# The second pass of the sample's attention scores as two 64-row matmuls side by side in the array

## The chip, the cores and the metric

The kernel runs on one core of one Trainium2 chip. The metric is the device time of one execution in microseconds (us); the median of three runs before the change is 1824.78 us (1824.75 to 1825.05). The engines are named as the profile names them: PE is TensorE (PEld its weight loads), DVE VectorE, ACT ScalarE, POOL GpSimd, SP the engine that issues the transfers.

## The reference, cut to what matters

One layer of a bidirectional encoder is applied to two sequences with the same weights, a prompt of 512 tokens and a sample of 1024. Width 1024, 8 query heads and 2 key/value heads of 64, MLP width 4096, all in float32.

```python
q = _axial_rope(_rmsnorm(q, q_g), ang_row, ang_col)
k = _axial_rope(_rmsnorm(k, k_g), ang_row, ang_col)
...
s = jnp.einsum('bqkgd,bskd->bkgqs', qi, k).astype(jnp.float32) * scale
p = jax.nn.softmax(s, axis=-1).astype(v.dtype)
return jnp.einsum('bkgqs,bskd->bqkgd', p, v)
...
h = h + jnp.concatenate([o_attn, o_pool], axis=-1) @ w_out
h = h + jnp.square(jax.nn.relu(m @ w_up)) @ w_down
```

The score of a query and a key is a product over the 64 numbers of a head. All sequences are attended to in full, without a mask.

## The kernel before, in words

Tokens are cut into 12 tiles of 128 (tiles 0 to 3 are the prompt, 4 to 11 the sample) and into three chunks of 512 (chunk 0 the prompt, 1 and 2 the sample). PE multiplies in the type float32r, which keeps fewer bits than float32. So every operand is stored as a high part (the rounded value) and a low part (the rest), and a product is made of several float32r products added up in PSUM.

For the scores the two parts are packed differently. A head has 64 numbers, the array 128 rows. `turn_qk` (line 327) writes the tile `qs` so that the high part of a head's q stands on 64 partitions and its low part on the other 64; heads with an even number have the high part on partitions 0 to 63, odd ones on 64 to 127. The tile goes to memory (`qs_d`), and `load_q` (line 402) brings it back as `qb`, one tile of tokens ahead of its use. The keys are stored as `ks[c][0]` (high part) and `ks[c][1]` (low part) of chunk c, and both repeat the head's 64 numbers on both halves of the partitions. One matmul over 128 rows of `qb` against `ks[c][0]` thus gives (q high + q low) times k high, a second one against `ks[c][1]` gives (q high + q low) times k low.

`Unit.score` (line 433) issues these for one head of one tile: for a prompt tile one chunk, two matmuls of 512 columns; for a sample tile two chunks, four matmuls, into one PSUM tile `S` of two banks. DVE then takes the row maximum (`nm`, line 441), ACT the exponentials (`soften`, 449), DVE the reciprocal of their sum, POOL the scaling (`norm`, 461), PE turns the weights (`turn`, tile `tp`), ACT and DVE split them (`split`, 472 and 473), PE multiplies them with v (`weigh`, tile `o`).

The order of all this is written out by hand in one loop (line 992), and PE, ACT, DVE and POOL execute it in that order. A unit is one tile and one key/value head, and each of its four steps handles one query head: in each step of the sample PE gets four score matmuls (`S`), four matmuls of `weigh` for work of earlier steps (`o`), eight transposes (`tp`) and, while there is such work, a piece of filling: six matmuls of the pooling heads' output projection (`pp`) or twelve of 256 columns of the attention heads' (`po`, lines 738 to 753). I call a step with a piece `po` filled and one without any unfilled. The sample has 8 tiles, 2 units each, 4 steps each: 64 steps.

Most tiles in the on-chip memory come from one pool of 49 equal slots (`slot`, line 74). All transfers are issued by SP, in order; `load` (line 55) also keeps a load behind the PE instruction before it in program order. Every matmul issued goes through `pe.matmul` (line 49), so the profile gives all of them that line and tells them apart by tile.

Of the kernel before, what the change touches and what calls it, by code (L numbers as in the profile page):

```python
# [10 lines left out]
F32R = mybir.dt.float32r  # L11
# [7 lines left out]
P = 128  # L19
# [3 lines left out]
NQ, NKV, HD = 8, 2, 64  # L23
# [3 lines left out]
SEQS = ((0, 4), (4, 8))  # L27
NT = 12
NF = 32
CH = 512  # L30
# [5 lines left out]
def encoder_layer(ctx, tc, xT, xn, xr, pT, w1, w2, w_pool, w_out, w_up, w_down, w_gate, w_proj,  # L36
# [18 lines left out]
    def load(dst, src):  # L55
        ins = sy.dma_start(dst, src).ins
        if last_pe[0] is not None:
            tc.add_manual_dep(ins, last_pe[0].name, NOSYNC, reason="not before its turn")

    def as32(ap):  # L60
        return ap.bitcast(F32)
# [12 lines left out]
    def slot(shape, dt, name):  # L74
        n = math.prod(shape[1:])
        full = slots.tile([P, SLOT], dt, tag="s", name=name)
        v = full[:, 0:n]
        if len(shape) == 3:
            v = v.rearrange("p (a b) -> p a b", a=shape[1])
        elif len(shape) == 4:  # L80
            v = v.rearrange("p (a b c) -> p a b c", a=shape[1], b=shape[2])
        return v

    def tp_ps(name):
        return pst.tile([P, CH], F32, tag="tp", name=name)
# [21 lines left out]
    qs_d = [dram.tile([P, NQ * P], F32, name=f"qs_d{t}") for t in range(NT)]  # L107
# [135 lines left out]
    ks, vs, uT = {}, {}, {}  # L243
# [153 lines left out]
        ve.scalar_tensor_tensor(y[:, 1], py, psc_sb[:, g:g + 1], as32(y[:, 0]), op0=ALU.mult, op1=ALU.subtract)  # L397
        sy.dma_start(yT_d[c][g], flat(y))

    qsb = {}  # L400

    def load_q(t):
        qsb[t] = slot([P, NQ, P], F32R, f"qb{t}")
        load(as32(qsb[t]).rearrange("p h t -> p (h t)"), qs_d[t])


    fill = deque()
# [12 lines left out]
    class Unit:  # L420
# [12 lines left out]
        def score(self, j, tag="s"):  # L433
            hq, nch = self.g * 4 + j, self.nc
            S = ps(tag, f"S{self.id}{j}") if tag == "s" else tp_ps(f"S{self.id}{j}")
            for c in range(nch):
                for i in range(2):
                    pe.matmul(S[:, c * CH:(c + 1) * CH], qsb[self.t][:, hq % 2 * 4 + hq // 2, :], ks[self.t0 // 4 + c][i][:, self.g, :],
                              start=i == 0, stop=i == 1)
            nm = small.tile([P, 1], F32, tag="nm", name=f"nm{self.id}{j}")  # L440
            ve.tensor_reduce(nm, S[:, :nch * CH], axis=AX.X, op=ALU.max, negate=True)
            self.S[j] = S, nm
# [448 lines left out]
    def stream():  # L891

        for n, pr in enumerate(pairs):
            for i, _ in enumerate(pr.feed()):
# [5 lines left out]

    unit = Unit(0, 0, 0)
    first = {(10, 6): [lambda: load_q(0)],
             (10, 7): [lambda: load_wo(4), lambda: load_wo(5)],
             (11, 0): [lambda: load_wo(6), lambda: load_wo(7)],
# [3 lines left out]
             (11, 4): [lambda: load_pool(0), lambda: load_h(0, 0), lambda: unit.norm(0), lambda: split_wo(6, ve)],  # L908
             (11, 5): [lambda: unit.score(1, "tp"), lambda: split_wo(7, ve)],
             (11, 6): [lambda: load_q(1)]}  # L910
    start_chunk(0)
    for k in range(KD - 2):
# [79 lines left out]
    for at in range(2, 4 * len(units) + 6):  # L992
        idx, j = divmod(at, 4)
        if j == 0:
            cur = Unit(*units[idx]) if idx < len(units) else None
            if cur and cur.g == 0 and cur.t + 1 < NT:
                load_q(cur.t + 1)
# [179 lines left out]
    for n, pair in enumerate(pairs):  # L1177
        c, g = pair.c, pair.g
# [215 lines left out]
```

## Time and profile before

| what | value |
|---|---|
| median of the runs | 1824.78 us |
| time of the profiled execution | 1827.95 us |
| its span, first to last instruction | 1826.2 us |
| PE busy | 1769.2 us, 97% |
| DVE busy | 1247.3 us, 68% |
| POOL busy | 1047.5 us, 57% |
| ACT busy | 939.5 us, 51% |
| granted TensorE clock, mean | 0.991 |
| score matmuls (`S`) | 320, from 181.9 to 542.8 us |

The profiled execution is one more run of the same program, 3.2 us above the median of the timed runs. Outside its span lie 1.75 us. A matmul's end is modelled in the profile, so durations of consecutive matmuls overlap; the pace of PE is read from the distance of starts. In a timeline the first number is the start and the second the length of a row of equal instructions, and the brackets say how long the engine had been idle and what it waited for.

### The profile page before, as it was taken

The page shows a single profiled execution, that of the slowest core. Times are in us where ns is not written, and L with a number is a line of the kernel's source. Part 1 is how long each engine was busy: PE and PEld are TensorE (multiplying, and loading weights), DVE is VectorE, ACT ScalarE, POOL GpSimd, SP SyncE. Part 2 cuts the span into 40 slices and gives each one's busy share as a digit, 9 for nine tenths or more (in the row PEclk, how much of TensorE's full clock was granted, in tenths as well). Part 3 has the DMA queues.
Part 4 walks back from the last instruction along what each step waited for, and adds up shares of the span by engine and source line. Part 5 has one row for each costly group of instructions (what it writes and reads, how often), then busy time and mean ns, then how long its engine had stood idle before and what let it go on. Part 6 is the DMA issues. An engine that isn't in the chain of part 4 may idle for free. (4 is left out here: it accounts for less than half of the span.)

```text
span 1826.2 us, 28559 instructions
## 1 busy us (share of the span) xinstructions
PE 1769.2 (97%) x10540; PEld 1543.7 (85%) x10540; DVE 1247.3 (68%) x1823; ACT 939.5 (51%) x1854; POOL 1047.5 (57%) x917
## 2 busy tenths in 40 slices
PE   9999899999998999999998999999999999999997
PEld 7888677888868898898987988898888898988787
DVE  5677865888894777755668777765776555665655
ACT  6333455768793456544445465545444544443332
POOL 3474774536574567866555668855576666543121
PEclk9999999999999999999999999999999999999998
DMA  6333544120619435533555425536442322272102
GB/s 246 116 131 110 198 170 176 36 93 18 214 41 366 154 122 183 192 110 101 179 217 202 150 93 196 184 111 243 164 141 93 110 98 93 93 260 69 58 12 81
DMA packets 83883, 256.84 MB, mean 141 GB/s; under 512 B 9888, under 2 KB 16416, under 8 KB 83744
## 3 DMA queue, kind: packets, MB, share of 16 engines
q1 hardware_dynamic: 83744, 255.02, 39.6%
q8 instruction: 83, 1.36, 0.3%
q14 instruction: 56, 0.46, 0.1%
HBM read 195.74 MB, written 59.24 MB: 140 GB/s over the span
## 5 line engine op out<-in xcount | busy, mean ns | idle before, releaser
L49 PE MATMUL pd<-r,wd 128*128 128x512 f32 x2304 | 572.2, 396 | 13.1 <-DVE r L885 11.8
L49 PEld LDWEIGHTS pd<-r,wd 128*128 128x128 f32 x2304 | 420.9, 189 | 104.5 <-DVE r L885 17.5
L786 POOL TENSOR_TENSOR w<-ws,w 128x512 fp32r<-128x512 f32 x192 | 269.5, 1408 | 232.3 <-ACT w L785 226.0
L786 POOL TENSOR_TENSOR w<-wur,w 128x512 fp32r<-128x512 f32 x144 | 212.8, 1488 | 141.8 <-ACT w L785 140.6
L836 DVE TENSOR_TENSOR h<-pd,h 128x1024 f32<-128x1024 f32 x192 | 233.8, 1217 | 86.4 <-PE pd L49 86.2
L785 ACT CAST w<-ws 128x512 fp32r<-128x512 f32 x192 | 118.5, 617 | 269.6 <-DVE ws L794 248.4
L461 POOL TENSOR_SCALAR pr<-pr,rr 128x512 f32<-128x512 f32 x160 | 111.1, 705 | 136.1 <-DVE rr L456 64.2
L49 PE MATMUL z<-w,x 128*128 128x512 f32 (+1 forms) x864 | 175.2, 359 | 0.5 <-DVE w L160 0.3
L816 DVE TENSOR_TENSOR wd<-wdr,wd 128x512 fp32r<-128x512 f32 x96 | 106.2, 1106 | 92.8 <-ACT wd L815 81.6
L49 PEld LDWEIGHTS pz<-mo,w 128*128 128x128 f32 x1152 | 151.6, 191 | 20.5 <-issue 12.4
L49 PEld LDWEIGHTS z<-w,x 128*128 128x128 f32 x864 | 143.0, 189 | 27.0 <-ACT w L159 2.0
L49 PE MATMUL pz<-mo,w 128*128 128x256 f32 x1152 | 154.9, 285 | 11.0 <-issue 8.9
L49 PE MATMUL pq<-mo,w 128*128 128x256 f32 x1152 | 154.2, 284 | 2.8 <-issue 2.0
L49 PE MATMUL px<-mo,w 128*128 128x256 f32 x1152 | 152.8, 282 | 0.0
L49 PEld LDWEIGHTS px<-mo,w 128*128 128x128 f32 x1152 | 147.0, 190 | 4.1
L49 PEld LDWEIGHTS pq<-mo,w 128*128 128x128 f32 x1152 | 144.8, 191 | 3.6 <-issue 3.6
L49 PE MATMUL pg<-hg,wg 128*128 128x512 f32 (+1 forms) x768 | 141.5, 339 | 0.2
L49 PEld LDWEIGHTS pg<-hg,wg 128*128 128x128 f32 x768 | 119.0, 188 | 18.0 <-DVE hg L1128 1.0
L472 ACT CAST pt<-tp 128x512 fp32r<-128x512 f32 x160 | 87.9, 591 | 88.9 <-PE tp L53 87.2
L816 POOL TENSOR_TENSOR wd<-wdr,wd 128x512 fp32r<-128x512 f32 x96 | 129.8, 1352 | 0.0
L473 DVE TENSOR_TENSOR pt<-tp,pt 128x512 fp32r<-128x512 f32 x160 | 104.1, 684 | 31.3 <-ACT pt L472 31.0
L885 DVE TENSOR_TENSOR r<-c,r 128x512 fp32r<-128x512 f32 x96 | 75.2, 788 | 72.6 <-ACT c L882 45.0
(195 smaller groups left out, 3021.6 us busy)
## 6 DMA issues: line engine op xcount, KB each, us to landing
wur<-in_w_up_dram SPq DMA_DIRECT2D x96, 512.0 KB, 4.1
wdr<-in_w_down_dram SPq DMA_DIRECT2D x96, 512.0 KB, 4.4
mo_d<-mm SPq DMA_DIRECT2D x84, 256.0 KB, 2.4
mo<-mo_d SPq DMA_DIRECT2D x42, 512.0 KB, 7.8
h_d<-h SPq DMA_DIRECT2D x16, 512.0 KB, 2.9
h<-h_d SPq DMA_DIRECT2D x16, 512.0 KB, 10.0
xn<-in_xn_dram SPq DMA_DIRECT2D x12, 512.0 KB, 6.3
qs_d<-qs SPq DMA_DIRECT2D x12, 512.0 KB, 3.0
```

The lines of the kernel that those rows point to most:

```text
L49: last_pe[0] = nc.tensor.matmul(*a, **k).ins
L461: gp.tensor_scalar(p, p, rr, 1.0, op0=ALU.mult, op1=ALU.mult)
L472: sc.copy(self.pt[kt][:, 0], tp)
L473: ve.tensor_tensor(self.pt[kt][:, 1], tp, as32(self.pt[kt][:, 0]), op=ALU.subtract)
L785: sc.copy(t[:, 0], x)
L786: gp.tensor_tensor(t[:, 1], x, as32(t[:, 0]), op=ALU.subtract)
L816: (gp, ve)[i].tensor_tensor(lo, self.dr[i][:, h], as32(hi), op=ALU.subtract)
L836: ve.tensor_tensor(h, pd.rearrange("p (a b) -> p a b", a=2), h, op=ALU.add)
L885: ve.tensor_tensor(self.r[i][:, 1], x, as32(self.r[i][:, 0]), op=ALU.subtract)
```

## The change

For sample tiles the loop over the passes is now outside the loop over the chunks. The first pass is unchanged, two matmuls over 128 rows with `ks[1][0]` and `ks[2][0]`. In the second pass each matmul has 64 rows: chunk 1 uses partitions 0 to 63, chunk 2 partitions 64 to 127. Both use a new tile `qh`, which holds the high part of q in both halves; so the second pass gives q high times k low, and the product of the two low parts is left out for the sample. The two 64-row matmuls lie in different row halves of the array and write different banks of `S`. `load_q` fills `qh` with four more transfers from `qs_d` for each of the 8 sample tiles.

```diff
     def load_q(t):
         qsb[t] = slot([P, NQ, P], F32R, f"qb{t}")
         load(as32(qsb[t]).rearrange("p h t -> p (h t)"), qs_d[t])
+        if t >= SEQS[1][0]:
+            qhi[t] = slot([P, NQ, P], F32R, f"qh{t}")
+            dst = as32(qhi[t]).rearrange("p h t -> p (h t)")
+            for half in (slice(0, HD), slice(HD, P)):
+                for e, src in enumerate((slice(0, HD), slice(HD, P))):
+                    load(dst[half, e * CH:(e + 1) * CH], qs_d[t][src, e * CH:(e + 1) * CH])
...
-            for c in range(nch):
-                for i in range(2):
-                    pe.matmul(S[:, c * CH:(c + 1) * CH], qsb[self.t][:, hq % 2 * 4 + hq // 2, :], ks[self.t0 // 4 + c][i][:, self.g, :],
-                              start=i == 0, stop=i == 1)
+            at = hq % 2 * 4 + hq // 2
+            for i in range(2):
+                for c in range(nch):
+                    rows, q = slice(0, P), qsb
+                    if i and nch == 2:
+                        rows, q = slice(c * HD, (c + 1) * HD), qhi
+                    pe.matmul(S[:, c * CH:(c + 1) * CH], q[self.t][rows, at, :],
+                              ks[self.t0 // 4 + c][i][rows, self.g, :], start=i == 0, stop=i == 1)
```

PE, in a filled step of tile 5, before the change: the end of a piece `po`, the four score matmuls, two of `weigh` and a pair of transposes. In the names, `ks1_0` is the high part of chunk 1's keys, `ks1_1` the low part.

```order
L49 MATMUL po03_3519<-cat0_0_2333,wo3_1_3324 128x256
L49 MATMUL S5_01_3537<-ks1_0_807,qb5_3145 128x512
L49 MATMUL S5_01_3537<-ks1_1_808,qb5_3145 128x512
L49 MATMUL S5_01_3537<-ks2_0_1404,qb5_3145 128x512
L49 MATMUL S5_01_3537<-ks2_1_1405,qb5_3145 128x512
L49 MATMUL o4_0_3395<-pt4_06_3513,vs2_1406 128x512 x2
```

The same place after the change:

```order
L49 MATMUL po03_3534<-cat0_0_2333,wo3_1_3334 128x256
L49 MATMUL S5_01_3552<-ks1_0_807,qb5_3150 128x512
L49 MATMUL S5_01_3552<-ks2_0_1404,qb5_3150 128x512
L49 MATMUL S5_01_3552<-ks1_1_808,qh5_3152 128x512
L49 MATMUL S5_01_3552<-ks2_1_1405,qh5_3152 128x512
L49 MATMUL o4_0_3405<-pt4_06_3528,vs2_1406 128x512 x2
```

The count of matmuls is the same, the middle two have changed places, and the last two read `qh` (their output, which the row shows, is still 128 by 512).

SP, where the query tiles 5 and 6 are loaded, before:

```order
L56 DMA qb5_3145<-qs_d5_78 128x1024
L56 DMA wor2_3216<-in_w_out_dram 128x1024
L56 DMA wor3_3296<-in_w_out_dram 128x1024
L735 DMA h_d2_3_315<-h23_3058 128x1024
L56 DMA qb6_3483<-qs_d6_79 128x1024
L707 DMA h_d0_0_304<-h00_1952 128x1024
```

And after:

```order
L56 DMA qb5_3150<-qs_d5_78 128x1024
L56 DMA qh5_3152<-qs_d5_78 64x512 x4
L56 DMA wor2_3226<-in_w_out_dram 128x1024
L56 DMA wor3_3306<-in_w_out_dram 128x1024
L745 DMA h_d2_3_315<-h23_3063 128x1024
L56 DMA qb6_3493<-qs_d6_79 128x1024
L56 DMA qh6_3495<-qs_d6_79 64x512 x4
L717 DMA h_d0_0_304<-h00_1952 128x1024
```

Four transfers of 64 by 512 stand behind each load of a sample tile's `qb`; what stood behind it follows them, in the same order.

## Rows read from the trace of the kernel before

**Rows 1.** The page's first part: busy time of each engine over the span, its share and the count of instructions.

```profile
PE 1769.2 (97%) x10540; PEld 1543.7 (85%) x10540; DVE 1247.3 (68%) x1823; ACT 939.5 (51%) x1854; POOL 1047.5 (57%) x917
```

**Rows 2.** Busy time of the engines in six stretches: the first sixteen filled steps, two unfilled ones, eight unfilled ones, the unfilled end of the sample, and the 40 us behind it. The columns are the stretch, its length, then busy time and count of PE, PEld, DVE, ACT and POOL, the granted clock of PE, the busy share of the DMA engines and GB/s.

```profile
326.00:393.00 67.00, 65.95 (x445) 59.29 (x444) 54.40 (x106) 45.08 (x108) 29.50 (x41) 1.00 0.13 46
393.00:399.00 6.00, 6.00 (x37) 5.15 (x36) 5.42 (x11) 4.83 (x13) 1.52 (x3) 1.00 0.73 261
432.00:457.00 25.00, 23.88 (x130) 17.87 (x129) 23.09 (x42) 23.09 (x56) 18.98 (x23) 1.00 0.03 11
491.00:544.00 53.00, 50.29 (x266) 36.99 (x264) 49.76 (x91) 49.04 (x117) 37.15 (x47) 1.00 0.24 91
560.00:580.00 20.00, 20.00 (x165) 19.52 (x164) 9.20 (x20) 4.25 (x8) 5.47 (x5) 1.00 1.02 389
580.00:600.00 20.00, 12.19 (x85) 11.97 (x84) 9.99 (x15) 5.74 (x12) 8.72 (x8) 0.77 1.00 402
```

**Rows 3.** The timeline of PE over two filled steps (start, length, instructions).

```profile
343.26 1.10 PE L49 MATMUL S<-ks,qb 128*128 128x512 f32 x4
344.20 1.09 PE L49 MATMUL o<-pt,vs 128*128 128x512 f32 x4
345.13 1.03 PE L53 MATMUL tp<-id_sb,pr 128*128 128x128 f32 x8
345.92 1.65 PE L49 MATMUL po<-cat,wo 128*128 128x256 f32 x12
347.41 1.09 PE L49 MATMUL S<-ks,qb 128*128 128x512 f32 x4
348.33 1.09 PE L49 MATMUL o<-pt,vs 128*128 128x512 f32 x4
```

**Rows 4.** The matmuls `po` in the stretch from 326 to 497 us, from the table of groups: count, busy time, mean length in ns, idle time of PE just before them. Under it the timeline of PE over the first sample steps, before that stretch and up to its beginning.

```profile
L49 PE MATMUL po<-cat,wo 128*128 128x256 f32 x384 | 53.4, 288 | 0.0
...
310.71 1.19 PE L49 MATMUL S<-ks,qb 128*128 128x512 f32 x4 [0.78 <-DVE h L733]
...
322.43 1.64 PE L49 MATMUL pp<-yb,wo 128*128 128x512 f32 x6
...
328.17 0.50 PE L49 MATMUL o<-pt,vs 128*128 128x512 f32 x1 [1.05 <-DVE pt L473]
```

**Rows 5.** The timeline of DVE in the filled step that begins at 343.26 us.

```profile
344.40 1.23 DVE L441 TENSOR_REDUCE nm<-S 128x1 f32<-128x1024 f32 x1 [0.52 <-PE S L49]
345.54 0.15 DVE L455 TENSOR_TENSOR rr<-sums 128x1 f32<-128x1 f32 x1
345.72 0.16 DVE L456 RECIPROCAL rr<-rr 128x1 f32<-128x1 f32 x1
346.43 1.29 DVE L473 TENSOR_TENSOR pt<-tp,pt 128x512 fp32r<-128x512 f32 x2 [0.55 <-ACT pt L472]
347.64 0.42 DVE L754 TENSOR_TENSOR h<-po,h 128x256 f32<-128x256 f32 x1
347.97 0.83 DVE L498 TENSOR_TENSOR ob<-o,ob 64x256 f32<-64x256 f32 x2
```

**Rows 6.** The timeline of PE over unfilled steps, in the last of the three unfilled stretches.

```profile
496.62 1.09 PE L49 MATMUL S<-ks,qb 128*128 128x512 f32 x4
...
499.34 1.10 PE L49 MATMUL S<-ks,qb 128*128 128x512 f32 x4
...
502.08 1.08 PE L49 MATMUL S<-ks,qb 128*128 128x512 f32 x4
503.49 1.25 PE L53 MATMUL tp<-id_sb,pr 128*128 128x128 f32 x8 [0.33 <-DVE pt L473]
504.50 1.17 PE L49 MATMUL o<-pt,vs 128*128 128x512 f32 x4
505.51 1.10 PE L49 MATMUL S<-ks,qb 128*128 128x512 f32 x4
507.19 1.25 PE L53 MATMUL tp<-id_sb,pr 128*128 128x128 f32 x8 [0.58 <-DVE pt L473]
```

**Rows 7.** The instructions on the tile `S`: shortest, median and longest duration in ns, first and last start in us.

```profile
L49 PEld LDWEIGHTS S<-ks,qb x320: 186/188/338, 181.9 to 542.5; 128*128 128x128 f32 x160
L49 PE MATMUL S<-ks,qb x320: 386/393/714, 181.9 to 542.8; 128*128 128x512 f32 x160
```

**Rows 8.** The transfers into `qb`: the issue on SP in ns with first and last start, and the time to landing.

```profile
L56 SPq DMA_DIRECT2D qb<-qs_d x12: 320/378/644, 176.4 to 492.2; - x12
DMA to landing us min/median/max: 3.3/4.1/8.6
```

**Rows 9.** What stands on SP behind the last load of `qb`, and where PE next needs it: the timeline of SP, then of PE.

```profile
492.24 0.38 SPq L56 DMA_DIRECT2D qb<-qs_d  x1
492.73 2.31 SPq L56 DMA_DIRECT2D h<-h_d  x4
...
548.89 1.67 PE L49 MATMUL po<-cat,wo 128*128 128x256 f32 x12
```

**Rows 10.** The longest stall of PE behind the sample's attention: the timeline of PE, then that of DVE.

```profile
585.81 1.58 PE L49 MATMUL pq<-mo,w 128*128 128x256 f32 x12
595.21 2.90 PE L49 MATMUL pz<-mo,w 128*128 128x256 f32 x12 [7.82 <-issue]
...
591.48 1.23 DVE L661 TENSOR_TENSOR h<-h,w 128x1024 f32<-128x1024 f32 x1 [9.54 <-DMA h_d<-h]
```

More of the change, by code (lines that the diff above doesn't have):

```diff
@@ L398, in pool_product @@
         sy.dma_start(yT_d[c][g], flat(y))
-    qsb = {}
+    qsb, qhi = {}, {}
     def load_q(t):
```

## The prediction

> **What bounds the kernel now.** I read the page's first part, then the busy time by stretch, then the timelines of PE and DVE over single steps. The page says that PE is busy 97% of the span [rows 1], so PE's own pace is what a change can win or lose almost everywhere. For the sample's attention that has to be seen step by step. In the first sixteen filled steps PE is busy 65.95 of 67 us, DVE 54.40, ACT 45.08 [rows 2]: PE sets the pace. A filled step lasts from one group `S` to the next, 343.26 to 347.41, 4.15 us, and PE goes through its four groups without a bracket of idle time [rows 3]. Read from the starts: four `S` 0.94 us (0.92 in the next step), so 0.233 us each; eight transposes 0.79 us, 0.099 each; twelve `po` 1.49 us. DVE does 1.23 + 0.15 + 0.16 + 1.29 + 0.42 = 3.25 us in such a step, in one of four 0.83 more, and it is DVE that waits for PE's `S` (0.52 us) and for ACT (0.55 us) [rows 5]. So there is room of about 0.7 us before DVE would take over.
>
> In unfilled steps it is the other way. They begin at 2.72 and 2.74 us (496.62, 499.34, 502.08), which is PE's own sum, and then stretch to 3.43 us with PE waiting 0.33 and 0.58 us for DVE's `pt` [rows 6]. DVE's work in such a step is 1.23 + 0.15 + 0.16 + 1.29, plus a quarter of 0.83, 3.04 us. In the eight steps from 432 us and in the end of the sample DVE is busy 23.09 of 25 and 49.76 of 53 us [rows 2]. There, a faster PE waits more and gains nothing.
>
> The number of filled steps: 384 matmuls `po` between 326 and 497 us, twelve a piece, 32 pieces [rows 4]. Of the other 32 sample steps four, from 310.71 us on, hold the last pooling pieces (to 322.43), and 28 are unfilled.
>
> **The change part by part.** *The first pass* keeps its two matmuls, 2 x 0.233 = 0.466 us. That they now stand next to each other changes no pace: within and between the groups of rows 3 the distance of starts stays at 0.23, whatever tile comes next.
>
> *The second pass* took 0.466 us. The trace of before has no matmul of 64 rows, so its cost is bounded from both sides. Lower end: both run fully side by side and the pair takes 0.233; gain 0.233 a step. Upper end: they overlap, but the array has to run empty when it goes from 128 rows to 64 and again when it goes back, with the weight load behind that exposed each time. The length of a matmul beyond the pace is 0.393 - 0.233 = 0.160 us, a weight load lasts 0.188 [rows 7]; two such changes are 2 x 0.348 = 0.696, so 0.233 + 0.696 - 0.466 = 0.463 lost, or 0.56 if the second load is not hidden either. Between these ends I go by the nearest row. Each of the 64-row matmuls has its own weight load, and PE takes load, matmul, load, matmul in order; a pair that is paced by its load and not by its columns is what the transposes show, 0.099 us. So the second matmul starts 0.099 behind the first and the pair takes 0.233 + 0.099 = 0.332. I take the change between row counts as free, since the step from float32r matmuls to transposes and back, another change of what the array does, costs nothing in rows 3. Gain 0.134 us a step.
>
> *Where it counts.* In 32 filled steps: 32 x 0.134 = 4.3 us. DVE's 3.25 to 4.1 us stays below 4.02 on average (3.46). In unfilled steps zero: they wait for DVE. In the four steps with pooling pieces I also take zero, for at 328.17, two steps behind them, PE waits 1.05 us for DVE [rows 4]; if it counted there, it were 0.5 us more.
>
> *The new transfers.* Per sample tile four issues of about 0.378 us, 1.5 us on SP [rows 8], in all 4 MB beside 255 MB. They are asked for a whole tile ahead, eight steps or some 30 us, and the same kind of transfer lands in 4.1 us, at most 8.6 [rows 8]. What stands behind them on SP moves back by 1.5 us: stores of h, weights of the output projection, and behind the last one the four loads of h issued at 492.73, which PE first needs at 548.89 [rows 9]. Cover is ample; without it the price would be a wait of a few us at one place. The new tile takes a slot for two tiles' time, at most two of 49 at once. I cost both at zero.
>
> *What comes after.* The gain must survive the stretch behind the attention. At 580 to 600 us PE is busy only 12.19 us, at a clock of 0.77, with the DMA engines full [rows 2]: PE stands for 7.82 us because DVE stands for 9.54 us on a transfer of h [rows 10]. These transfers are issued behind PE's and POOL's work of the attention, so I let the whole stretch move forward with it.
>
> The sum, against the profiled execution: 1827.95 - 4.3 = 1823.6 us. That execution is 3.2 us above the median of the runs, so for the timed runs 1824.8 - 4.3 = 1820.5 us.
>
> The Trainium skill, page "TensorE: Matmul & The Clock Gate", section "Measured speedup vs the span model", gives 3.07 times for four matmuls of 32 rows packed in one array, with a start some 4 ns apart; by that, as an estimate, the pair would take nearly one matmul's time and the sum would be the lower end, some 7 us. No run here shows it yet.
>
> **The rivals.** *Changing the row count empties the array.* One group of four becomes two matmuls of 128 rows, two of 64, then 128 again: two changes in every sample step, 128 in all. If only the matmul's tail of 0.160 is exposed each time, a step costs 0.332 + 0.320 - 0.466 = 0.186 more. In 36 PE-bound steps 6.7 us, and in unfilled steps, where PE's 2.73 becomes 2.92 beside DVE's 3.04, at most half of it again, 28 x 0.09 = 2.5: together about +8, 1833 us with a part of that. At the upper end of the price (+0.56 a step) it is 36 x 0.56 = 20, and unfilled steps go from 3.13 (25 us for eight, rows 2) to 2.73 + 0.56 = 3.29, 4.5 more: 1849 us. It decides from 0.067 us a change on, since two of these eat the 0.134. For it: the pace of 0.233 rests on the next load and the next matmul running into the one before, and nothing shows that this holds between different row counts. Against it: the free passage from matmul to transpose [rows 3]. The Trainium skill states this rule outright: in "TensorEngine Tiling (Array Packing)", section "Key Properties", changing the tiling mode, not just the tile, drains TensorE. The trace cannot confirm it, as no matmul of before has another mode; it is why this rival's chance is high.
>
> *The two matmuls don't overlap*, or the changes eat just what the overlap gives. Then the same four matmuls take the same time and the result is 1824.8 us. For it: matmuls of before run strictly one after another. Against it: the two use different rows and banks.
>
> *The gain is taken back at 587 us.* If the full DMA engines, not the attention's end, date the end of DVE's 9.54 us wait [rows 10], PE only waits longer there: 1824.8 us again. For it: share 1.02 and 1.00 [rows 2]. Against it: before 546 us these engines are mostly idle, so the burst begins when the attention lets it.
>
> **How the numbers follow.** Overlap with cheap changes 0.46; emptying the array 0.35; no overlap 0.14; taken back 0.05. The first spreads from 1816.4 (0.233 in 36 steps) to about 1822.5, and 0.40 of its 0.46 lies below 1821.1, which is 0.2% (3.65 us) under the median and about what a measurement of this kernel can tell from no change. The second lies above 1828.4 with 0.31, and 0.04 inside. So faster 0.40, same 0.06 + 0.04 + 0.14 + 0.05 = 0.29, slower 0.31. Since both signs are likely, the range is wide: 1816.8 to 1836, which leaves out the expensive end of emptying (0.10) and a little of the best case; the likeliest case's own range is 1817 to 1822.5.
>
> **What would show it.** In the timeline of PE over a filled step, the four `S` should take 0.80 us instead of 0.93 up to the next group's start, and the step 4.02 instead of 4.15, with the last two `S` starting about 0.1 us apart. Starts 0.23 apart show no overlap. A gap before the third `S` and before the first `o` behind them, a longer step and more idle PE would show emptying. The unfilled stretches should last as before (25 and 53 us), with more of PE's waits on DVE. DVE's idle time on `S` should shrink. The stall of 7.82 us should keep its length. A wait of PE on a transfer to `qh` would show that the transfers are not hidden. A change of other stages by more than 1 us would mean that the reading of the shift is wrong.

## The result, and the profile after

The changed kernel takes 1833.52 us (median of 6 runs, 1830.10 to 1835.44) against 1824.76 us for the kernel before in the same comparison (6 runs, 1821.34 to 1827.20). The ratio is 1.0047, 95% interval 1.0032 to 1.0061: slower by 6 to 11 us, where 4.3 us of gain was forecast. The profiled execution took 1834.45 us.

First the busy times over the span, as in [rows 1].

```profile
PE 1774.5 (97%) x10540; PEld 1527.1 (83%) x10540; DVE 1245.9 (68%) x1823; ACT 940.1 (51%) x1854; POOL 1047.8 (57%) x917
```

Nothing stands out: the other engines do the same work in a longer span, PE stays at 97%. The answer is in the single step. The timeline of PE over a filled step and the beginning of the next, to be laid beside [rows 3]:

```profile
346.60 0.62 PE L49 MATMUL S<-ks,qb 128*128 128x512 f32 x2
347.15 0.50 PE L49 MATMUL S<-ks,qh 64*128 64x512 f32 x2
347.57 1.19 PE L49 MATMUL o<-pt,vs 128*128 128x512 f32 x4
348.61 1.03 PE L53 MATMUL tp<-id_sb,pr 128*128 128x128 f32 x8
349.40 1.66 PE L49 MATMUL po<-cat,wo 128*128 128x256 f32 x12
350.89 0.63 PE L49 MATMUL S<-ks,qb 128*128 128x512 f32 x2
```

Read from start to start. The step lasts 4.29 us instead of 4.15; the median of the 32 filled steps is 4.32 against 4.16. The first pass, two matmuls of 128 rows, takes 0.55 until the 64-row pair starts; it had 0.466. The pair takes 0.42 until the next group; it had 0.466. The four `o` behind it take 1.04; they had 0.93. `tp` and `po` are as before. So the pair itself is hardly shorter, and both neighbours of it became longer. No row has a bracket: PE waits for no other engine. The weight loads of the same place show where the time goes:

```profile
346.48 0.31 PEld L49 LDWEIGHTS S<-ks,qb 128*128 128x128 f32 x2
347.14 0.19 PEld L49 LDWEIGHTS S<-ks,qh 64*128 64x128 f32 x2 [0.36 <-issue]
347.57 0.76 PEld L49 LDWEIGHTS o<-pt,vs 128*128 128x128 f32 x4 [0.24 <-ACT pr L459]
```

And the same engine in the kernel before, in the step of [rows 3] that begins at 343.26:

```profile
343.14 0.79 PEld L49 LDWEIGHTS S<-ks,qb 128*128 128x128 f32 x4
343.97 0.89 PEld L49 LDWEIGHTS o<-pt,vs 128*128 128x128 f32 x4
```

Before, the loads of `o` begin at 343.97, 0.23 us ahead of the first `o` at 344.20. After, the load of the 64-row pair begins at 347.14 with its matmul at 347.15, and that of `o` at 347.57 with its matmul at 347.57: neither is brought forward, and the load queue stands 0.36 and 0.24 us before them. (The releaser written beside 0.24 is an ACT instruction; at the same place one step on, at 351.88, the same 0.24 stands with "issue", so I don't read it as a wait for ACT.) The instructions on the tile `S`, as in [rows 7], and the sum of that idle time:

```profile
L49 PE MATMUL S<-ks,qb x192: 387/395/504, 181.8 to 546.0; 128*128 128x512 f32 x192
...
L49 PEld LDWEIGHTS S<-ks,qh x128: 182/183/183, 309.7 to 546.3; 64*128 64x128 f32 x128
L49 PE MATMUL S<-ks,qh x128: 491/492/502, 309.7 to 546.3; 64*128 64x512 f32 x128
...
  issue: 23.3, 64
```

Two matmuls of 492 ns are listed as 0.50 us together, so they start within about 10 ns of each other: they do run side by side. The loads stand still 64 times ahead of the pair, once a score, 0.36 us each.

The unfilled steps, as in [rows 6], start every 2.83 to 2.85 us instead of 2.72 to 2.75 and then reach the same pace of DVE. The eight-step stretch, first of before and then of after, from its first score to that of the next filled step:

```profile
432.14 1.09 PE L49 MATMUL S<-ks,qb 128*128 128x512 f32 x4
...
457.34 1.08 PE L49 MATMUL S<-ks,qb 128*128 128x512 f32 x4
```

```profile
434.41 0.63 PE L49 MATMUL S<-ks,qb 128*128 128x512 f32 x2
...
459.81 0.63 PE L49 MATMUL S<-ks,qb 128*128 128x512 f32 x2
```

25.20 us became 25.40. The busy times of the 40 us behind the attention, which answer to the last two lines of [rows 2], and the stall of [rows 10]:

```profile
564.00:584.00 20.00, 20.00 (x162) 19.57 (x161) 8.85 (x19) 4.25 (x8) 5.65 (x5) 1.00 0.97 374
584.00:604.00 20.00, 11.73 (x82) 11.52 (x82) 9.73 (x15) 5.62 (x11) 8.14 (x8) 0.77 1.02 409
```

```profile
599.62 2.90 PE L49 MATMUL pz<-mo,w 128*128 128x256 f32 x12 [8.27 <-issue]
```

The stall keeps its form, 8.27 us instead of 7.82, and stands 4.4 us later. The stretch moves with the attention's end. The transfers into the new tile, for [rows 8]:

```profile
L56 SPq DMA_DIRECT2D qh<-qs_d x32: 445/594/1217, 272.9 to 498.3; - x32
...
DMA to landing us min/median/max: 2.8/4.4/10.8
```

An issue costs SP 0.594 us at the median, more than the 0.378 of a whole tile, though it moves a quarter of the bytes. No engine waits for one of these transfers.

For what follows I use one length that holds everything the change touches: from the first score of the sample (the `S` behind PE's 0.78 us wait for `h`) to the first `px`. The rows of before, then of after:

```profile
310.71 1.19 PE L49 MATMUL S<-ks,qb 128*128 128x512 f32 x4 [0.78 <-DVE h L733]
...
580.11 1.59 PE L49 MATMUL px<-mo,w 128*128 128x256 f32 x12
```

```profile
309.01 0.73 PE L49 MATMUL S<-ks,qb 128*128 128x512 f32 x2 [0.78 <-DVE h L743]
...
584.06 1.59 PE L49 MATMUL px<-mo,w 128*128 128x256 f32 x12
```

269.40 us became 275.05, 5.65 us more. Counted from one group `S` to the next, the 32 filled steps hold 4.1 us of it (134.8 to 138.9 us in all), the four steps with pooling pieces 0.5; the rest is spread over the unfilled steps and the end.

### The profile page after: what moved, and what is told of

Its sections match the earlier page's. It is cut to its first block, busy times and chain, and to the rows that moved or that the text cites. A ratio compares the mean times of both kernels' runs of the same rounds, so it can differ in the third digit from the quotient of the medians.

```text
span 1832.6 us, 28630 instructions
## 1 busy us (share of the span) xinstructions
PE 1774.5 (97%) x10540; PEld 1527.1 (83%) x10540; DVE 1245.9 (68%) x1823; ACT 940.1 (51%) x1854; POOL 1047.8 (57%) x917
## 4 chain that ended last, share of the span: by engine, by line
PE 52%; DVE 6%; DMA 4%; ACT 4%; issue 3%; POOL 2%; SPq 0%; DVEq 0%; POOLq 0%; ACTq 0%
PE pd L49 23%; PE pg L49 6%; PE px L49 6%; PE pz L49 6%; PE pq L49 5%; PE py L49 3%; PE pj L49 2%; POOL w L796 1%; DVE h L846 1%; DVE r L895 1%; ACT w L795 1%; DVE h L671 1%; DMA mo_d<-mm 1%; DMA w<-w_d 1%; DVE wd L826 1%
```

## The experiments

My theory after the result: the pair does overlap fully and gains one matmul's 0.233 us, but each change between 128 and 64 rows costs about 0.19 us (0.233 + 0.15 = 0.385 for two): the next load is not brought forward and, as I take it, the array runs empty first. The rivals: the new transfers and slots are the cost; the 64-row matmuls are slow by themselves; the new order costs. All comparisons below are with the kernel before on the same chip in the same batch (medians 1826.64, 1826.60 and 1826.19 us).

**Full rows again, everything else kept.**

```diff
                     if i and nch == 2:
-                        rows, q = slice(c * HD, (c + 1) * HD), qhi
+                        q = qhi
```

> The new tile, its four transfers a tile and the new order of the passes stay; only the second pass uses all 128 rows again (with the high part of q on both halves, so the product with the keys' low part is counted twice and q's low part is left out of it: the numbers change, the work of every engine is that of before). My theory: the loss sits in the two changes of the row count in each score, about 0.19 us each, against 0.233 us that the overlap gives back; without them a filled step takes 4.15 us again, the eight-step unfilled stretch 25.2 us, and the whole 1824 to 1826 us. Rival: the transfers and the shifted slots cost what the attention steps don't explain (8.8 us by the medians, some 5.4 us in the sample's steps); then filled steps take 4.15 us and the whole still 1827.5 us or more.

Measured: ratio 1.0012 (1.0003 to 1.0021), 1828.33 us. A filled step has its old form, `S` two by two in 0.92 us and 4.13 us from 343.88 to 348.01:

```profile
343.88 0.62 PE L49 MATMUL S<-ks,qb 128*128 128x512 f32 x2
344.34 0.62 PE L49 MATMUL S<-ks,qh 128*128 128x512 f32 x2
344.80 1.08 PE L49 MATMUL o<-pt,vs 128*128 128x512 f32 x4
345.72 1.03 PE L53 MATMUL tp<-id_sb,pr 128*128 128x128 f32 x8
346.51 1.66 PE L49 MATMUL po<-cat,wo 128*128 128x256 f32 x12
348.01 0.62 PE L49 MATMUL S<-ks,qb 128*128 128x512 f32 x2
```

The length from the first sample score to `px` is 269.5 us. So the row count alone makes the loss in the attention. But the whole is some 0.5 to 4 us above the kernel before and outside the 1824 to 1826 us that the theory had: the rival holds a small part.

**Both matmuls on the same rows.**

```diff
                     if i and nch == 2:
-                        rows, q = slice(c * HD, (c + 1) * HD), qhi
+                        rows, q = slice(0, HD), qhi
```

> Both matmuls of the second pass use partitions 0 to 63 (the keys' low part stands on both halves, so the result is the same), so they cannot run side by side; the row count still changes twice. My theory (full overlap in the changed kernel, worth 0.233 us, and two changes at 0.19): the second pass takes 0.233 us longer than in the changed kernel, a filled step 4.54 us, and as an unfilled step then has 3.1 us of PE work, hardly more there; the whole 1838 to 1842 us. Rival (the 64-row matmuls do not overlap on the chip and are slow by themselves): a filled step stays at 4.31 us and the whole at 1833 us.

Measured: ratio 1.0101 (1.0088 to 1.0115), 1845.02 us. The upper edge of what was expected was 1842; taken against its own batch, where the kernel before stands 1.9 us higher than in the first comparison, it lies 18.4 us up instead of 13 to 17, and 15.6 of them lie between the first sample score and `px`.

```profile
346.08 0.63 PE L49 MATMUL S<-ks,qb 128*128 128x512 f32 x2
346.64 0.73 PE L49 MATMUL S<-ks,qh 64*128 64x512 f32 x2
347.30 1.20 PE L49 MATMUL o<-pt,vs 128*128 128x512 f32 x4
```

The second pass takes 0.66 us to the next group instead of 0.42, 0.24 more, which is one matmul's pace; its neighbours are the same 0.56 and 1.03. The filled step (346.08 to 350.62 us) is 4.54 us, as expected. So the overlap in the changed kernel is real and worth a whole matmul, and the price lies at its two edges. The rival, slow 64-row matmuls that don't overlap, is out.

As the two don't overlap here, each change can be read by itself. The same rows one matmul at a time, and the second weight load of the 64-row pair:

```profile
346.31 0.40 PE L49 MATMUL S<-ks,qb 128*128 128x512 f32 x1
346.64 0.49 PE L49 MATMUL S<-ks,qh 64*128 64x512 f32 x1
346.98 0.39 PE L49 MATMUL S<-ks,qh 64*128 64x512 f32 x1
347.30 0.50 PE L49 MATMUL o<-pt,vs 128*128 128x512 f32 x1
347.63 0.40 PE L49 MATMUL o<-pt,vs 128*128 128x512 f32 x1
...
346.75 0.19 PEld L49 LDWEIGHTS S<-ks,qh 64*128 64x128 f32 x1
```

The starts lie 0.32 to 0.34 us apart, where the pace is 0.233. So entering costs some 0.09 us ahead of the first 64-row matmul and 0.10 behind it, where its own load is not hidden, and leaving costs the same two again: 0.19 us each way. Inside the pair the second load stands 0.23 us ahead of its matmul, though it uses the same rows; it is at the change of the row count that loads are held back.

**All four matmuls of 64 rows.** This leaves out the product of q's low part with the keys' high part.

```diff
-                    if i and nch == 2:
+                    if nch == 2:
                         rows, q = slice(c * HD, (c + 1) * HD), qhi
```

> The first pass too is two 64-row matmuls with the high part of q; the product of q's low part with the keys' high part is left out. Still two changes of the row count a score, but two pairs side by side. My theory (the price is one for each change, none for each pair): the four matmuls take 2 x 0.233 + 2 x 0.19 = 0.85 us, a filled step 4.07 us, the whole 2 to 3 us under the kernel before, some 1822 us. Rival (each 64-row pair costs its 0.42 us, as the one in the changed kernel does from its start to the next group): two pairs 0.85 us, a filled step 4.15 to 4.2 us, the whole 1825 to 1827 us.

Measured: ratio 0.9981 (0.9969 to 0.9993), 1822.77 us, 3.9 us under the kernel before.

```profile
347.00 0.73 PE L49 MATMUL S<-ks,qh 64*128 64x512 f32 x4
347.69 1.16 PE L49 MATMUL o<-pt,vs 128*128 128x512 f32 x4
348.69 1.03 PE L53 MATMUL tp<-id_sb,pr 128*128 128x128 f32 x8
349.48 1.67 PE L49 MATMUL po<-cat,wo 128*128 128x256 f32 x12
351.07 0.73 PE L49 MATMUL S<-ks,qh 64*128 64x512 f32 x4
```

Two pairs take 0.66 to 0.69 us up to the next group where one took 0.42. So a second pair costs 0.24 to 0.27, about one matmul's pace, and not another 0.42. The price belongs to the change of the row count and not to the pair. The step is 4.07 us, as the theory had it (the median of the 32 is 4.09), and the stretch from the first sample score to `px` is 2.8 us shorter than before. With the same two changes a score, four matmuls' work in two matmuls' time is just enough to win. It isn't a replacement: it computes less.

**The changed kernel again.** The edit is none.

> The changed kernel once more, beside the others. My theory: filled steps 4.31 us, the sample's attention 5.4 us longer than before; the whole 5 to 7 us above the kernel before, since the rest of the 8.8 us between the medians is spread between runs. Rival: the whole is again 8 us or more above, and the part behind the attention is longer by 3 us in every execution.

Measured: ratio 1.0040 (1.0027 to 1.0053), 1833.61 us, 7.0 us above the kernel before. From the first sample score to `px` it takes 275.2 us, 5.8 more than before; from the first `px` to the last `pd`, the MLP, 1057.6 us (586.2 to 1643.8) where the kernel before had 1057.4 (580.1 to 1637.6) and the first profile of the changed kernel 1060.6. So the 3 us by which that profile was longer behind the attention were one execution's, and the rival that they come every time is out.

**Only the new order.**

```diff
-            for c in range(nch):
-                for i in range(2):
-                    pe.matmul(S[:, c * CH:(c + 1) * CH], qsb[self.t][:, hq % 2 * 4 + hq // 2, :], ks[self.t0 // 4 + c][i][:, self.g, :],
+            at = hq % 2 * 4 + hq // 2
+            for i in range(2):
+                for c in range(nch):
+                    rows, q = slice(0, P), qsb
+                    pe.matmul(S[:, c * CH:(c + 1) * CH], q[self.t][rows, at, :],
```

> Only the new order of the passes (pass outside chunk); no new tile, no new transfers, all matmuls of 128 rows on the old tile. My theory: the order costs nothing and the small rest that the full-row version kept (1.0012) belongs to the transfers or to the slots that the new tile shifts; so a filled step takes 4.15 us and the ratio to the kernel before is 1.0000 within 0.001. Rival: the order itself costs the rest, and the ratio stays at 1.001 or more.

Measured: ratio 1.0002 (0.9991 to 1.0014), 1827.60 us; filled steps 4.13 to 4.18 us as before (the first of each run of them apart); 269.4 us from the first sample score to `px`. The order is free.

**Two heads share one pair of changes.** In steps with an even head the first pass of two heads, then their second pass as two pairs; the odd head's score step keeps only its maximum. The product of the two low parts is left out, as in the changed kernel. The loop issues the scores of such a step behind the transposes.

```diff
+                if j % 2 == 0:
...
+                    for c in range(nch):
+                        for h in (j, j + 1):
+                            hh = self.g * 4 + h
+                            rows = slice(hh % 2 * HD, (hh % 2 + 1) * HD)
+                            pe.matmul(self.S[h][:, c * CH:(c + 1) * CH], qsb[self.t][rows, hh % 2 * 4 + hh // 2, :],
+                                      ks[self.t0 // 4 + c][1][rows, self.g, :], start=False, stop=True)
```

> Another use of the 64-row pairs: two heads share one pair of changes. In every second step of the sample PE issues the first pass of two heads (four matmuls of 128 rows) and then their second pass as four 64-row matmuls, the even head on partitions 0 to 63 and the odd one on 64 to 127, where the old tile already has each head's high part; so no new tile and no transfer. In steps with an even head the scores stand behind the transposes. My theory: two steps save 2 x 0.233 us and pay two changes at 0.19, so two filled steps take 8.3 - 0.08 = 8.22 us (the same place with all rows: 8.30), and the whole is 0.1 to 1.5 us below its own control with full rows; whether it beats the kernel before depends on waits that the new order brings for the score tiles, which I put at 0 to 6 us. Rival: each 64-row pair pays for itself, so two pairs cost 2 x 0.155 us more and two filled steps take 8.6 us, 5 us more in the whole than the control.

**Its control, all rows.**

```diff
-                            rows = slice(hh % 2 * HD, (hh % 2 + 1) * HD)
+                            rows = slice(0, P)
```

> The control of the run before it: same order, two heads at once, but the second pass over all 128 rows. My theory: two filled steps take 8.30 us; the whole 0.1 to 1.5 us above the two-head version with 64 rows, and 0 to 6 us above the kernel before. Rival: 5 us below the two-head version with 64 rows.

Measured: ratio 1.0200 (1.0187 to 1.0214) and 1.0196 (1.0183 to 1.0209), 1862.67 and 1862.25 us. Both are 36 us slower than the kernel before, far beyond the 0 to 6 us that I gave the new order, and a difference between them of 0.1 to 1.5 us is lost in their intervals. The waits in the stretch from 320 to 560 us of the first show what the order does:

```profile
ACT pr L464 <- DVE nm L456: 58.9, 28, 3.5
```

ACT now waits 58.9 us for the row maxima, which come two at a time behind late scores. The steps in which PE itself waits for nothing still answer the question. First the control, then the 64-row version, over two filled steps:

```profile
354.40 2.10 PE L49 MATMUL S<-ks,qb 128*128 128x512 f32 x8
...
362.69 1.64 PE L49 MATMUL S<-ks,qb 128*128 128x512 f32 x6
```

```profile
355.94 1.84 PE L49 MATMUL S<-ks,qb 128*128 128x512 f32 x8
...
364.14 1.17 PE L49 MATMUL S<-ks,qb 128*128 128x512 f32 x4
```

Two steps take 8.29 us with all rows and 8.20 with two pairs. Five such pairs of the 64-row version run without a wait of PE and at the full granted clock, in 8.20 to 8.25 us, those of the control in 8.29 to 8.32: some 0.07 less, where the theory had 0.08 and the rival 0.3 more. One pair of changes for two heads just pays for itself, at a price for the order that nobody would pay.

**What is left: the new tile and its transfers.** Once more full rows, first with one transfer into the new tile instead of four, then unchanged.

```diff
-            for half in (slice(0, HD), slice(HD, P)):
-                for e, src in enumerate((slice(0, HD), slice(HD, P))):
-                    load(dst[half, e * CH:(e + 1) * CH], qs_d[t][src, e * CH:(e + 1) * CH])
+            load(as32(qhi[t]).rearrange("p h t -> p (h t)"), qs_d[t])
```

> The full-row version once more, with the new tile filled by one transfer of 128 by 1024 instead of four of 64 by 512 (it then holds what the old tile holds, so the second pass is that of the kernel before): same bytes, same slot, a quarter of the issues. If the small rest (ratio 1.0012 for the full-row version) lies in the issues on SP, the ratio falls to 1.000; if it lies in the slot and the bytes, it stays near 1.001. The stretch from the first sample score to the first px stays at 269.5 us in either case.

> The full-row version with four transfers again. If its ratio of 1.0012 was real, it comes out between 1.0005 and 1.002 again; if it was spread between runs, near 1.000. The stretch from the first sample score to the first px is 269.5 us again.

Measured: 1.0011 (1.0002 to 1.0020) and 1.0006 (0.9997 to 1.0015); the stretch of the attention is 269.7 and 269.4 us. So nothing points at the number of issues, but these intervals are too wide to rule it out. Three comparisons with the tile lie 0.06 to 0.12% above the kernel before, some 1 to 2 us, and the one without it at 0.02%; the intervals overlap. A small cost of the tile is likely, it is not in the attention, and where it arises stays open.

## Why the prediction was wrong

- *What bounds the kernel:* right. The loss is there in filled steps, where PE sets the pace (4.16 to 4.32 us, 4.1 us of the 5.65 in all 32), and nearly absent in unfilled ones, where DVE does (25.20 to 25.40 us for eight). The four steps with pooling pieces, which I had at zero, lost 0.5 us.
- *The second matmul starts 0.099 behind the first:* wrong, and in the good direction. The pair starts together, and its two loads lie over each other too (0.19 us for both, against 0.31 for two ordinary loads). Two side by side take about one matmul's time, as the second pair of the version with four shows. The lower end of my range for the pair held.
- *The step that failed:* "I take the change between row counts as free, since the step from float32r matmuls to transposes and back, another change of what the array does, costs nothing in rows 3." The change costs about 0.19 us, twice a score: 0.09 more up to the pair, 0.19 in the pair's own 0.42 (one matmul's pace is 0.233), 0.11 more in the group behind it, against a gain of 0.233. A transpose uses the array in the same row count, so its free passage said nothing on this. I had both prices as ends and chose between them by the wrong likeness.
- *The rival "changing the row count empties the array"* is the one that the runs bear out. That the change of the row count is what costs, where, and how much is shown by the two experiments that keep both changes and alter what runs between them, and by the one that takes them away. That the array itself is empty in these 0.09 us no row shows, since the ends of matmuls are modelled; the load that is held back shows. Its cheap price, 0.160 a change with 0.099 for the second matmul, made +0.186 us a step; it is +0.15 to 0.17, from 0.19 a change and no delay, and the 0.19 is a short wait and a half-hidden load, not a matmul's tail. Its time of 1833 us meets the measured 1833.52 partly by luck: of its 9 us I had up to 2.5 in the unfilled steps, where the stretch of eight lost 0.2, and the whole holds 1 to 2 us of the new tile that I had at zero.
- The Trainium skill states both halves of this. "TensorEngine Tiling (Array Packing)", section "Key Properties", has the drain on a change of tiling mode: the trace fits it, with 0.19 us for each change, though the drain itself has no row. "TensorE: Matmul & The Clock Gate", section "Measured speedup vs the span model", has packed matmuls starting almost together: the trace agrees, within 10 ns.
- *The transfers:* no engine waited for one, as said, though an issue took SP 0.594 us and not the 0.378 that I reckoned with. That the tile cost nothing at all is not confirmed.
- *The gain taken back at 587 us:* the stall moved with the attention's end (595.21 to 599.62) and grew by 0.45 us, so the reading that this stretch shifts was right, for a loss.
- *The chances:* slower had 0.31, less than faster with 0.40. A cost without any row in the trace, which the Trainium skill's rule on a change of tiling mode puts on the other side, deserved the larger share. The stated range holds 1833.52 us only because it was made wide enough for both signs.

## What to carry to other kernels

Two 64-row matmuls on different row halves and PSUM banks really do run in one matmul's time, but entering and leaving that mode costs about 0.19 us each way here, so a block has to replace at least two 512-column matmuls before it wins (one saved lost 0.15 to 0.17 us a step, two saved won 0.07 to 0.08). Group all the narrow work of several outputs between one entry and one exit, and count the entries before writing it. Where the trace has no example of an operation, a likeness to another free transition is no price: measure one step of it first.

## What the runs showed of the hardware that I had not expected

- A 64-row matmul is listed at 492 ns against 393 to 395 for one of 128 rows, because its load is not brought forward and starts with it (the second one of the same-rows version, whose load is ahead, is listed at 0.39 us); two of them on different halves together are listed at 0.50 us, and 0.73 us on the same half.
- At a change of the row count PE's load queue stands: 64 times ahead of the pair, 23.3 us in all, 0.36 us each, and the profile shows nothing that it waits for.
- A transfer of 64 by 512 costs SP 0.594 us to issue at the median, one of 128 by 1024 0.378.
- One and the same program varies by several us between executions (1821.34 to 1827.20 for the kernel before), and the MLP stretch of the changed kernel was 1060.6 and 1057.6 us in its two profiles. A difference of 3 us between two single profiles proves nothing here; the step lengths, repeated 32 times in one execution, do.
